# Encoder trunk on one core: in the down-projections of the gated MLP, two weight chunks of each half go through Strassen's seven block products; weights come in half-chunks, and PSUM is handed out bank by bank

## The chip, the core and the metric

The kernel runs on one core of one Trainium2 chip. The engines are TensorE (PE, matrix products), VectorE (DVE), ScalarE (ACT), GpSimd (POOL) and SyncE (SP, which here issues most of the transfers). The metric is the device time of one execution in microseconds (us); lower is better. Before the change three runs gave 2313.19, 2313.24 and 2313.95 us; the median is 2313.24.

## What is computed

A trunk of two layers on 256 tokens of width 2048. Layer 0 has grouped-query attention (mixer A), layer 1 a mixture of dilated windows (mixer B); a gated MLP of inner width 5632 follows each. All of it is float32.

```python
h = x
for i in range(DEPTH):                       # DEPTH = 2
    hn = rms_norm(h, mix_norm[i])
    h = h + (mixer_a if i % 2 == 0 else mixer_b)(hn, ...)
    h = h + conv_ffn(rms_norm(h, ffn_norm[i]), w_up[i], conv_w[i], conv_b[i], w_down[i])
return rms_norm(h, final_norm)

def conv_ffn(h, w_up, conv_w, conv_b, w_down):
    u = h @ w_up                             # 2048 -> 2 x 5632
    u = depthwise_conv_over_positions(u, conv_w, width 3) + conv_b
    gate, val = split(u)
    return (silu(gate) * val) @ w_down       # 5632 -> 2048
```

## The kernel before

**Products.** Float32 accuracy is made of three products of a rounded format: a weight tile `raw` is rounded on ACT to `wh`, DVE subtracts to get the rest `wl`, and activations are kept as a pair of tiles in the same way (`xh` and `xl`, for the MLP's inner values `ah` and `al`). Each K tile of 128 rows then takes wh by xh, wl by xh and wh by xl. The stationary operand is the activation, 128 tokens wide (token block m = 0 or 1); the moving operand is a weight row of 512 columns (n = 0 to 3 for the 2048 outputs); the sum lies in one PSUM bank of 128x512.

**Weights.** A chunk `kg` is 512 rows by 512 columns, 1 MB. `feed` (L114) loads it in one transfer on SP's queue into one of three `raw` buffers, and splits it in two half-chunks of two K tiles each. The pairs `wh`, `wl` turn in a ring of three (`NHL`). The two split instructions are placed ahead of their position in the text by `tc.high_priority(offset=AHEAD)`, 45 instructions. `feed_T` (L90) does the same for the up-projection, where the weight is the stationary operand: 16 matmuls (8 of 512 columns, 8 of 256) for each kg. Instructions of an engine run in one order, which the framework makes from the order of the text, the priorities and its own estimate of what is ready.

**The MLP** (`ffn`, L291). It runs in two halves, of six and of five groups p of 512 inner columns (`HALVES`). In each half the up-projection comes first: for each p and each hh (256 columns) the accumulators `ga` and `va`, two banks each, are fed; `up_post` (L327) takes them out of PSUM (L334 on ACT, L335 on DVE), scales, convolves, and `glu` (L353) multiplies gate by value on POOL (L354) and splits the product into `ah` and `al` (L178, L179). This side work stands in a list of generators, `pending`, of which `step()` runs one piece after each half-chunk or kg of weights. Then the half's down-projection: `project2` for n = 0 and 1 together, with the last kg of both at the end (the last product of the up-projection is still to be finished then, and `drain()` ends it before that kg), then `project` for n = 2 and n = 3. `done` adds the accumulators to the residual `h` (L273; L396 in the last half of layer 1, where the final norm follows). In a second half of layer 0 it also starts the transposes for the next layer.

**PSUM.** Eight banks: a pool of four accumulators (`accp`), taken two at a time by `new_acc`, so that a new pair takes the banks of the pair before the last; and a pool of four for everything else (`ps_tile`).

**Side inputs.** In layer 0 `bias_lines` (L664) makes bias tables beside the up-projection: small matmuls, copies to `ln` on DVE, and stores to DRAM on SP's queue (L685). In layer 1 `fin` is the final norm's gain, loaded by POOL at the start of the MLP.

## Time and profile before

| | us |
|---|---|
| median of three runs | 2313.24 |
| span of the profiled execution | 2312.0 |
| TensorE busy | 2292.1 |
| VectorE busy | 1613.9 |
| ScalarE busy | 1210.7 |
| GpSimd busy | 162.4 |
| down-projection of layer 0: first half, six chunks | from 546.6 to 677.2 |
| down-projection of layer 0: second half, five chunks | from 900.65 |
| last matmul | 2303.0 |

The profile is of one execution. A group of instructions is given by the line in the kernel, the engine, the operation and its tiles (output, arrow, inputs), with the number of instructions, their busy time, the mean duration of one in ns, and the idle time of the engine before them with what ended it. Matmuls overlap in the pipeline: the duration of one is longer than the interval at which they are issued. A row of the timeline is start, duration, engine, line, tiles, and in brackets the idle time before it and its releaser. A row of the table by stretches gives start and end, then length, and for each engine busy time and number of instructions, the granted TensorE clock, the DMA share and GB/s.

### The profile page before, as it was taken

To read this page: it belongs to the slowest core of one execution; us is meant where nothing else is said; L and a number is where in the kernel's file an instruction comes from. 1 tells how busy PE (TensorE), PEld (TensorE's weight loads), DVE (VectorE), ACT (ScalarE), POOL (GpSimd) and SP (SyncE) were. 2 spreads that over 40 slices of the span, in tenths; PEclk is the share of its full clock that TensorE was granted. 3 is DMA by queue.
4 is the path that set the end of the run, shared out by engine and by line. 5 is a ranking of instruction groups with operands and counts; after the bars stand their busy time and mean duration, and the time that the engine had idled before them with its cause. 6 is when DMAs were issued, how large, how long until landed. Compare 5 with 4: busy or idle time off the path is not lost.

```text
span 2312.0 us, 30191 instructions
## 1 busy us (share of the span) xinstructions
PE 2292.1 (99%) x11641; PEld 1946.0 (84%) x11641; DVE 1613.9 (70%) x2321; ACT 1210.7 (52%) x1746; POOL 162.4 (7%) x127
## 2 busy tenths in 40 slices
PE   9999999999999999999999999999999999999998
PEld 7788788888888888888888888878888888888886
DVE  6877877676457776778776876586777754677755
ACT  6565565554345555455454554445555543555543
POOL 2210000010000010010000000000101100001010
PEclk9999999999999999999999999999999999999999
DMA  8444565665555555565555554556555555555554
GB/s 289 156 146 148 190 201 180 229 201 194 187 195 191 191 184 189 181 222 200 195 178 174 174 198 164 172 190 212 186 191 190 191 186 198 191 191 183 193 190 146
DMA packets 229024, 437.46 MB, mean 189 GB/s; under 512 B 10400, under 2 KB 193440, under 8 KB 201104
## 3 DMA queue, kind: packets, MB, share of 16 engines
q1 hardware_dynamic: 226976, 429.82, 55.2%
q0 software_dynamic: 1472, 5.15, 0.7%
q8 instruction: 91, 1.49, 0.3%
q10 hardware_dynamic: 432, 0.56, 0.1%
q14 instruction: 53, 0.43, 0.0%
HBM read 429.20 MB, written 6.29 MB: 188 GB/s over the span
## 4 chain that ended last, share of the span: by engine, by line
PE 89%; DVE 6%; DMA 2%; issue 1%; POOL 1%; ACT 1%; SPq 1%; POOLq 0%; DVEq 0%; ACTq 0%
PE acc L107 26%; PE acc L128 15%; PE acc L129 15%; PE acc L127 15%; PE acc L110 14%; DVE wl L140 2%; DVE tT L219 2%; DMA raw<-in_w_up_dram 2%; PE ps L190 1%; PE ps L194 1%; PE ps L193 0%; PE ps L192 0%; POOL t L576 0%; SPq L685 0%; DVE h L273 0%
## 5 line engine op out<-in xcount | busy, mean ns | idle before, releaser
L140 DVE TENSOR_TENSOR wl<-raw,wh 128x1024 fp32r<-128x1024 f32 (+1 forms) x456 | 552.6, 1214 | 333.1 <-ACT wh L139 329.5
L139 ACT ACTIVATE wh<-raw 128x1024 fp32r<-128x1024 f32 (+1 forms) x456 | 475.1, 1044 | 545.6 <-PE acc L129 494.5
L107 PE MATMUL acc<-xh,wh 128*128 128x512 f32 x2816 | 707.5, 393 | 3.1 <-ACT wh L102 3.0
L107 PEld LDWEIGHTS acc<-xh,wh 128*128 128x128 f32 x2816 | 507.1, 189 | 95.7 <-ACT wh L102 4.1
L103 DVE TENSOR_TENSOR wl<-raw,wh 128x1024 fp32r<-128x1024 f32 x352 | 431.7, 1228 | 202.1 <-ACT wh L102 191.7
L102 ACT ACTIVATE wh<-raw 128x1024 fp32r<-128x1024 f32 x352 | 372.1, 1058 | 311.1 <-PE acc L107 204.4
L110 PEld LDWEIGHTS acc<-xh,wl 128*128 128x128 f32 x2816 | 384.1, 190 | 27.5
L128 PE MATMUL acc<-wl,ah 128*128 128x512 f32 x1024 | 400.1, 391 | 2.5 <-DVE wl L140 2.2
L127 PE MATMUL acc<-wh,ah 128*128 128x512 f32 x1024 | 399.2, 390 | 0.0
L129 PE MATMUL acc<-wh,al 128*128 128x512 f32 x1024 | 398.8, 389 | 0.0
L110 PE MATMUL acc<-xh,wl 128*128 128x256 f32 x2816 | 392.6, 282 | 0.0
L127 PE MATMUL acc<-wh,xh 128*128 128x512 f32 x768 | 302.3, 394 | 0.9 <-ACT wh L139 0.9
L128 PE MATMUL acc<-wl,xh 128*128 128x512 f32 x768 | 300.3, 391 | 2.2 <-DVE wl L140 2.1
L129 PE MATMUL acc<-wh,xh 128*128 128x512 f32 x768 | 299.6, 390 | 0.0
L128 PEld LDWEIGHTS acc<-wl,ah 128*128 128x128 f32 x1024 | 192.3, 188 | 46.5 <-DVE wl L140 7.6
L127 PEld LDWEIGHTS acc<-wh,ah 128*128 128x128 f32 x1024 | 192.3, 188 | 39.7
L129 PEld LDWEIGHTS acc<-wh,al 128*128 128x128 f32 x1024 | 192.3, 188 | 39.4
L354 POOL TENSOR_TENSOR cv<-cg,cv 128x512 f32<-128x512 f32 x44 | 95.5, 2170 | 1165.4 <-DVE cv L346 975.4
L128 PEld LDWEIGHTS acc<-wl,xh 128*128 128x128 f32 x768 | 144.4, 188 | 32.6 <-DVE wl L140 5.3
L129 PEld LDWEIGHTS acc<-wh,xh 128*128 128x128 f32 x768 | 144.2, 188 | 29.9
L127 PEld LDWEIGHTS acc<-wh,xh 128*128 128x128 f32 x768 | 144.4, 188 | 29.4 <-ACT wh L139 1.7
L178 ACT ACTIVATE ah<-cv 128x256 fp32r<-128x256 f32 x88 | 32.0, 411 | 105.1 <-POOL cv L354 105.1
(152 smaller groups left out, 1374.8 us busy)
## 6 DMA issues: line engine op xcount, KB each, us to landing
raw<-in_w_up_dram SPq DMA_DIRECT2D x352, 512.0 KB
raw<-in_w_down_dram SPq DMA_DIRECT2D x88, 1024.0 KB
raw<-in_w_b_dram SPq DMA_DIRECT2D x72, 1024.0 KB
raw<-in_w_bo_dram SPq DMA_DIRECT2D x24, 1024.0 KB
raw<-in_w_a_dram SPq DMA_DIRECT2D x16, 1024.0 KB
raw<-in_w_ao_dram SPq DMA_DIRECT2D x16, 1024.0 KB
raw<-in_w_a_dram SPq DMA_DIRECT2D x16, 256.0 KB
raw<-in_w_a_dram SPq DMA_DIRECT2D x8, 512.0 KB
```

The lines of the kernel that those rows point to most:

```text
L102: nc.scalar.activation(wh, rk, AF.Copy)
L103: nc.vector.tensor_tensor(wl, rk, wh.bitcast(F32), ALU.subtract)
L107: nc.tensor.matmul(acc[j], wh[:, kt, j * P:(j + 1) * P], lhs[4 * kg + kt][2], start=first and i == 0 and kt == 0, stop=False)
L110: nc.tensor.matmul(acc[j][:, :NT], wl[:, kt, j * P:(j + 1) * P], lhs[4 * kg + kt][0], start=False, stop=end and kt == 3)
L127: nc.tensor.matmul(accs[m], xh[:, c], wh[:, j, :], start=st, stop=False)
L128: nc.tensor.matmul(accs[m], xh[:, c], wl[:, j, :], start=False, stop=False)
L129: nc.tensor.matmul(accs[m], xl[:, c], wh[:, j, :], start=False, stop=sp)
L139: nc.scalar.activation(wh[:, c], r[:, c], AF.Copy)
L140: nc.vector.tensor_tensor(wl[:, c], r[:, c], wh[:, c].bitcast(F32), ALU.subtract)
L178: nc.scalar.activation(hi, src, AF.Copy)
L219: nc.vector.transpose(o[cols].rearrange("p a (m t) -> p a m t", m=2)[:, :, :, rows], s[rows].rearrange("p m (a c) -> p a m c", c=P)[:, :, ...
L354: nc.gpsimd.tensor_tensor(cv, cg, cv, ALU.mult)
```

## The change

A chunk of the inner values is a matrix of 2 token blocks by 2 K halves, and the weights of a chunk for two n are 2 K halves by 2 columns of blocks. Multiplied directly that is 8 block products, of 6 matmuls each (2 K tiles, 3 products). The changed kernel does the chunks 0 and 2 of each half (`SKG`) by a form of Strassen's scheme with 7 block products: four raw half-chunks are summed in place on DVE (`prepare`), the activations are held in seven forms, sums and differences of their blocks, each split in a pair (`glu_forms`), and the products M1, M5, M6, M7 have banks of their own beside C11, C12, C21, C22, eight in all. `combine` puts the four M into the residual. This is done for n = 0, 1 in both halves, and for n = 2, 3 in the first half only; in the second halves n = 2 and n = 3 go through `project` as before, from the forms that are the plain blocks (an eighth form is added there).

The seven P units of a Strassen chunk are mixed with the four units c of a chunk multiplied directly, in the order `MIX`; chunks that are left follow as c units: eight in a first half, four in a second. In the pair (0, 1) `drain()` stands before the last four units.

Beside that: `raw` is six half-chunks with a list of free ones, loaded by transfers of half the size, everywhere in the kernel; the `wh`, `wl` ring gets a fourth pair while a down-projection runs (tags `wh9`, `wl9`, which bias_lines uses before); banks are named, accumulators take 0 to 3 by turns of two and `ps_tile` 4 to 7; `fin` is loaded in four parts at the last down-projection, into tiles of the up-projection's input; `bias_lines` uses tiles of the MLP's pool, and one `ln` in place of two.

The diff, cut to its core:

```diff
-NRAW, NHL = 3, 3
+NRAW, NHL = 6, 3
+SKG = (0, 2)
+MIX = (("P", 1), ("c", 0), ("P", 2), ("P", 5), ("c", 1), ("P", 3), ("P", 7), ("c", 2), ("P", 6), ("P", 4), ("c", 3))
...
-    accp = ctx.enter_context(tc.tile_pool(name="accp", bufs=4, space=PS))
-    psp = ctx.enter_context(tc.tile_pool(name="psp", bufs=4, space=PS))
+    psp = ctx.enter_context(tc.tile_pool(name="psp", bufs=1, space=PS))
...
+    def bank(i, name):
+        return psp.tile([P, 512], F32, tag=f"b{i}", name=nm(name))
...
+        bank_at[1] = (bank_at[1] + 1) % 4
+        return bank(4 + bank_at[1], "ps")
...
+    def split_raw(r, release=True):
+        wh, wl = new_hl()
+        with tc.high_priority(offset=AHEAD):
+            nc.scalar.activation(wh, r, AF.Copy)
+            nc.vector.tensor_tensor(wl, r, wh.bitcast(F32), ALU.subtract)
+        if release:
+            done_raw(r)
+        return wh, wl
...
     def new_acc():
-        return [accp.tile([P, 512], F32, tag="acc", name=nm("acc")) for _ in range(2)]
+        bank_at[0] = (bank_at[0] + 2) % 4
+        return [bank(bank_at[0] + m, "acc") for m in range(2)]
...
+    def project_pair(w, n0, n1, lhs, forms, units, late, early_done, n0_done):
+        home = {1: "M1", 2: "C11", 3: "C12", 4: "C21", 5: "M5", 6: "M6", 7: "M7"}
+        place = ("M1", "M5", "M6", "M7", "C11", "C21", "C12", "C22")
+        acc = {k: bank((4, 5, 6, 7, 0, 1, 2, 3)[i], "acc") for i, k in enumerate(place)}
...
+        sums = {5: ("11", "12"), 7: ("12", "22"), 6: ("22", "11"), 4: ("21", "22")}
...
+        def prepare(u):
+            kind, kg, p = u
+            if kind == "P" and p in sums:
+                dst, src = (block(kg, b) for b in sums[p])
+                with tc.high_priority(offset=AHEAD):
+                    nc.vector.tensor_tensor(dst, dst, src, ALU.add)
+                if p == 6:
+                    done_raw(blocks.pop((kg, "11")))
+                elif p == 4:
+                    done_raw(blocks.pop((kg, "22")))
+
+        last_s = max(i for i, u in enumerate(units) if u[0] == "P")
+        for i, (kind, kg, p) in enumerate(units):
+            if i == late:
+                drain()
+            if kind == "c":
+                r = load_raw(w, (n0, n1)[p // 2], kg, p % 2)
+            else:
+                b = {1: "11", 2: "21", 3: "22", 5: "11", 7: "12", 6: "22", 4: "21"}[p]
+                r = block(kg, b)
+            if i + 1 < len(units):
+                prepare(units[i + 1])
+            wh, wl = split_raw(r, kind == "c" or p in (7, 4))
...
+            for k, xh, xl, j in todo:
+                nc.tensor.matmul(acc[k], xh, wh[:, j, :], start=k in fresh, stop=False)
+                fresh.discard(k)
+                nc.tensor.matmul(acc[k], xl, wh[:, j, :], start=False, stop=False)
+            todo.sort(key=lambda t: (t[0], t[3]))
+            for k, xh, xl, j in todo:
+                nc.tensor.matmul(acc[k], xh, wl[:, j, :], start=False, stop=last[k] == i and j == 1)
+            if i == last_s:
+                early_done(acc)
+            if i == last["C21"]:
+                n0_done(acc)
+            step()
...
+            def glu_forms(cg, cv, fm, hh):
+                nc.gpsimd.tensor_tensor(cv, cg, cv, ALU.mult)
+                yield
...
+                if hh == 0:
+                    kept[0] = cv
+                    put(1, cv[:, :, :P])
+                    if 0 in fm:
+                        put(0, cv[:, :, P:])
+                    s3 = tmp()
+                    nc.vector.tensor_tensor(s3, cv[:, :, :P], cv[:, :, P:], ALU.subtract)
+                    yield
+                    put(7, s3)
+                    return
+                c0 = kept.pop(0)
+                s1, s2, s4 = tmp(), tmp(), tmp()
+                nc.vector.tensor_tensor(s1, cv[:, :, P:], c0[:, :, P:], ALU.subtract)
+                put(2, cv[:, :, :P])
+                nc.vector.scalar_tensor_tensor(s2, s1, -1.0, c0[:, :, :P], ALU.mult, ALU.subtract)
+                yield
+                put(5, s1)
+                put(4, cv[:, :, P:])
+                nc.vector.tensor_tensor(s4, cv[:, :, :P], s2, ALU.add)
+                yield
+                put(6, s2)
+                put(3, s4)
...
-                done(project2(wd, 0, 1, slots, list(range(np_)), 1, lambda a: done(a, 0)), 1)
-                for n in (2, 3):
-                    done(project(wd, n, slots, list(range(np_)), last and hf == 1 and n == 3), n)
+                if last and hf == 1:
+                    for n in range(4):
+                        f = hpool.tile([P, 512], F32, tag=f"x{n}", name=nm("fin"))
+                        nc.gpsimd.dma_start(f, final_norm[n * 512:(n + 1) * 512].partition_broadcast(P))
+                        fin.append(f)
+                ckg = [k for k in range(np_) if k not in SKG]
+                units = []
+                for k in SKG:
+                    c = ckg.pop(0)
+                    units += [("c", c, u[1]) if u[0] == "c" else ("P", k, u[1]) for u in MIX]
+                units += [("c", c, i) for c in ckg for i in range(4)]
+                hl_ring.insert(0, (fp, 9))
...
+                def combine(acc, n0, n1):
+                    u, v = (fp.tile([P, 512], F32, tag="v", name=nm("cu"), bufs=2) for _ in range(2))
+                    nc.scalar.activation(u, acc["M1"], AF.Copy)
+                    nc.vector.tensor_tensor(hcol(0, n0), acc["M1"], hcol(0, n0), ALU.add)
+                    yield
+                    nc.vector.tensor_tensor(u, acc["M6"], u, ALU.add)
+                    nc.vector.tensor_tensor(v, acc["M5"], u, ALU.add)
+                    yield
+                    nc.vector.tensor_tensor(u, acc["M7"], u, ALU.add)
+                    nc.vector.tensor_tensor(hcol(0, n1), hcol(0, n1), v, ALU.subtract)
+                    yield
+                    nc.vector.tensor_tensor(hcol(1, n0), hcol(1, n0), u, ALU.add)
+                    yield
+                    nc.vector.tensor_tensor(u, acc["M5"], u, ALU.add)
+                    nc.vector.tensor_tensor(hcol(1, n1), hcol(1, n1), u, ALU.subtract)
+
+                def pair(n0, n1, late):
+                    acc = project_pair(wd, n0, n1, slots, forms, units, len(units) - 4 if late else None,
+                                       lambda a: start(combine(a, n0, n1)),
+                                       lambda a: done((a["C11"], a["C21"]), n0))
+                    done((acc["C12"], acc["C22"]), n1)
+
+                pair(0, 1, True)
+                if hf == 0:
+                    pair(2, 3, False)
+                else:
+                    seq = [k for k in range(np_)]
+                    for n in (2, 3):
+                        done(project(wd, n, slots, seq, last and hf == 1 and n == 3), n)
+                hl_ring.remove((fp, 9))
```

More of the change, by code (lines that the diff above doesn't have):

```diff
@@ L185, in split_scaled, with at @@
         nc.vector.scalar_tensor_tensor(lo, src, sc, hi.bitcast(F32), ALU.mult, ALU.subtract)
+    def at(e, m):
+        return e[m] if isinstance(e, list) else tuple(t[:, m * P:(m + 1) * P] for t in e[:2])
     def mm3(o, lhsT, rhs, ls, rs, start, stop):
@@ new lines, in ffn @@
+                for p in range(p0, p1):
+                    if p - p0 in SKG:
+                        fm = forms[p - p0] = {f: new_form() for f in (1, 7, 2, 5, 4, 6, 3) + (0,) * hf}
+                        if hf:
+                            for kt in range(4):
+                                slots[4 * (p - p0) + kt] = [
+                                    tuple(t[:, kt % 2 * P:(kt % 2 + 1) * P] for t in fm[f])
+                                    for f in ((1, 0), (2, 4))[kt // 2]]
+                    else:
+                        slots.update({4 * (p - p0) + j: new_form() for j in range(4)})
```

149 lines of the change are left out of this document (101 added, 48 removed).

## The prediction

> **What bounds the kernel now.** I read the page first: busy shares, the clock in the slices, the chain that ended last.
>
> ```profile
> span 2312.0 us, 30191 instructions
> PE 2292.1 (99%) x11641; PEld 1946.0 (84%) x11641; DVE 1613.9 (70%) x2321; ACT 1210.7 (52%) x1746; POOL 162.4 (7%) x127
> PEclk9999999999999999999999999999999999999999
> PE 89%; DVE 6%; DMA 2%; issue 1%; POOL 1%; ACT 1%; SPq 1%; POOLq 0%; DVEq 0%; ACTq 0%
> ```
>
> PE is busy 99% of the span at the full clock and carries 89% of the chain. So a matmul less is worth its issue interval, provided that nothing else leaves PE idle. Next I cut out the down-projection of layer 0's first half, and its groups.
>
> ```profile
> 546.60:677.20 130.60, 130.60 (x578) 108.15 (x577) 66.31 (x64) 52.39 (x54) 2.17 (x1) 1.00 0.57 193
> L127 PE MATMUL acc<-wh,ah 128*128 128x512 f32 x192 | 74.7, 389 | 0.0
> L128 PE MATMUL acc<-wl,ah 128*128 128x512 f32 x192 | 74.7, 389 | 0.0
> L129 PE MATMUL acc<-wh,al 128*128 128x512 f32 x192 | 74.7, 389 | 0.0
> L140 DVE TENSOR_TENSOR wl<-raw,wh 128x1024 fp32r<-128x1024 f32 x46 | 56.4, 1226 | 60.8 <-ACT wh L139 60.7
> L139 ACT ACTIVATE wh<-raw 128x1024 fp32r<-128x1024 f32 x46 | 48.8, 1061 | 72.7 <-PE acc L129 70.0 <-PE acc L107 1.7 <-ACT cv L339 0.7
> ```
>
> The first row gives length, then busy time of PE, PEld, DVE, ACT, POOL, then clock, DMA share, GB/s. 3x192 = 576 matmuls fill 130.6 us with PE never idle: 0.2267 us each (389 ns is the latency of one; they overlap). One half-chunk (2 K tiles, two token blocks, 3 products) is 12 matmuls, 2.72 us. ACT rounds it (1.061), DVE subtracts (1.226), and ACT then waits for PE to give a buffer back: the splits run a whole ring ahead, and DVE is used 66.31 of 130.60 us.
>
> **What it takes off PE.** A chunk with two n is 48 matmuls directly and 7 block products x 6 = 42 by Strassen's scheme. Two chunks in each pair of n; pairs (0,1) and (2,3) in a first half, only (0,1) in a second: 3 pairs x 2 chunks x 2 layers = 12 times 6 = 72 matmuls, 72 x 0.2267 = **16.3 us**. The six matmuls of a product go to one bank in a row; three in a row do now at that same interval, so I keep it (no run of six is in the trace; in the up-projection the banks alternate, and four 512-wide matmuls there, in a row below, take 1.07 us, 0.39 for one and (1.07-0.39)/3 = 0.227 for each more, so either order costs the same).
>
> **What it adds to the splits.** Eleven units (7 P, 4 c) are 42 + 48 = 90 matmuls, 20.4 us. DVE gets 11 subtractions and 4 sums of raw blocks. A sum in place of that size is in the trace, in mixer A:
>
> ```profile
> L578 DVE TENSOR_TENSOR ro<-ro,t 128x1024 f32<-128x1024 f32 x5 | 6.1, 1217 | 0.8 <-POOL t L576 0.8
> ```
>
> 11x1.226 + 4x1.217 = 18.4 us on DVE against 20.4 us on PE, 90%. ACT has 11x1.061 = 11.7. On average DVE keeps pace, with 2.0 us to spare per stretch (pitch below: more). In detail: a P unit gives PE 1.36 us, a P with a sum asks DVE for 2.44. But the order never has more than two P together, and with the fourth hl pair a split may run three units ahead; the three units ahead of any unit hold at least one c, so at least 1.36+1.36+2.72 = 5.4 us. The chain of one unit is sum, rounding, subtraction: 1.217+1.061+1.226 = 3.5 us. I take **0** here. Its bounds are 0 and, if nothing ran ahead, the slower rival's price below. The c units behind both stretches (8 or 4) need DVE 1.23 of 2.72 us and rebuild the lead.
>
> The first pair meets the last gated product's work too. Rows of DVE, ACT and PE at the start of that stage:
>
> ```profile
> 546.62 0.40 PE L127 MATMUL acc<-wh,ah 128*128 128x512 f32 x1
> 545.91 1.06 ACT L139 ACTIVATE wh<-raw 128x1024 fp32r<-128x1024 f32 x1 [1.72 <-PE acc L107]
> 546.88 0.64 ACT L334 ACTIVATE v<-acc 128x256 f32<-128x256 f32 x2
> 547.01 1.23 DVE L140 TENSOR_TENSOR wl<-raw,wh 128x1024 fp32r<-128x1024 f32 x1 [1.56 <-ACT wh L139]
> 548.15 0.75 DVE L335 TENSOR_TENSOR v<-acc,v 128x256 f32<-128x256 f32 x2
> 548.93 0.69 DVE L337 TENSOR_TENSOR u<-v,rbc 128x512 f32<-128x512 f32 x1
> 551.80 0.88 DVE L344 SCALAR_TENSOR_TENSOR cv<-u,cw,cv 128x256 f32<-128x256 f32 x2
> 552.59 0.87 DVE L346 SCALAR_TENSOR_TENSOR cv<-u,cw,cv 128x256 f32<-128x256 f32 x2
> 553.43 1.23 DVE L140 TENSOR_TENSOR wl<-raw,wh 128x1024 fp32r<-128x1024 f32 x1
> 553.64 2.17 POOL L354 TENSOR_TENSOR cv<-cg,cv 128x512 f32<-128x512 f32 x1 [21.01 <-DVE cv L346]
> 556.29 0.76 DVE L179 TENSOR_TENSOR al<-cv,ah 128x256 fp32r<-128x256 f32 x2 [1.63 <-ACT ah L178]
> ```
>
> A subtraction holds DVE 547.01 to 548.15 = 1.14 us when the next follows at once, so fifteen take 17.1 us and leave 3.3. The extra work is 0.75+0.69+0.88+0.87+0.76 = 4.0 us, over two stretches with 6.6 us free. Covered. The product is wanted only by the last four units, 2 x 20.4 us later.
>
> **New wait one: the start of a pair.** Before, four accumulators rotated. Now C11 lies in bank 0, where va was, and unit c0 comes second. P1 ends at 546.62 + 1.36 = 547.98. Bank 0 is free when the first L335 is done, 548.15 + 0.38 = 548.53, and with 0.07 us for the signal (an estimate: from ACT's end, 545.91 + 1.06, to DVE's start at 547.01 it is 0.04) c0 starts at 548.60: 0.62 us late. Bank 1 is free at 548.15 + 0.75 + 0.07 = 548.97, and C11's first two matmuls have issued by 549.05: no more. Four starts: **2.5 us**. Bounds: 0, if DVE takes L335 ahead of the subtraction; (0.62+1.14) x 4 = 7.0, if a second subtraction or sum stands ahead. I take the order that the trace has. Late next is nothing: all later units shift with it, and the splits gain lead.
>
> **New wait two: the end of a pair.** C12 and C22 lie in banks 2 and 3, and the next accumulator (ga of the second half, or the acc of n = 2) takes just these. Today's end of that stage:
>
> ```profile
> 676.92 1.28 DVE L273 TENSOR_TENSOR h<-acc,h 128x512 f32<-128x512 f32 x2
> 677.21 1.07 PE L107 MATMUL acc<-xh,wh 128*128 128x512 f32 x4
> ```
>
> The residual adds take DVE from 676.92 to 678.20, 0.64 each, and PE went on at 677.21 into other banks. Now the first matmul waits for 677.56+0.07, 0.42 late. In feed_T the second writes bank 3, free at 678.27 instead of wanted at 677.86: 0.41 more. Two such ends: 1.7 us. With n = 2, three matmuls (0.68) go to bank 2 first, so 0.42; but there DVE has the combine (8 more operations like L273, 8x0.64 = 5.1 us), the C11 adds and, in layer 0, transposes, all within c3 and four c units, 13.6 us, that need 5 x 1.14 of DVE besides. That is tight, so I take 0.8 each, 1.6. Sum **3.3 us**; bounds 0 and 3.3 + 4x1.14 = 7.9 (a subtraction ahead each time). In first halves eight c units, 21.8 us, hide the combine.
>
> **What is hidden, and by what.** *Forms.* Seven or eight splits in place of four, and four sums or differences, per Strassen chunk, in the up-projection:
>
> ```profile
> 677.20:901.00 223.80, 223.80 (x1283) 196.97 (x1282) 161.55 (x233) 127.80 (x186) 20.14 (x9) 1.00 0.58 189
> ```
>
> At 0.38 us for a 256-wide DVE operation (half of L179's pair) the most is 2x(4+4)x0.38 = 6.1 us per half, in 62 us of idle DVE; without that cover, 4 x 6.1 = 24 us. *Loads.* Twice as many of half the size on SP; volume and order stay, the stage moves 193 GB/s at a DMA share of 0.57, and eight half-chunks per 20.4 us instead of 21.8 ask 7% more: 0.61. Slots: in a stretch four raws are held by blocks, and walking through the list of free ones, each load's slot was given back by a split five or more units earlier, at least 3x1.36 + 2x2.72 = 9.5 us. *fin.* Four POOL issues ahead of the last product, 4 x 0.75 = 3.0 us, hidden by the 40 us above:
>
> ```profile
> L711 POOL DMA_DIRECT2D btg<-scr x4 | 3.0, 747 | 86.8 <-DVE lg L745 86.8
> oh<-in_onehot_dram POOLq DMA_DIRECT2D x1, 512.0 KB, 3.9
> ```
>
> *bias_lines.* Its stores share SP with the weights and hold them up today:
>
> ```profile
> PE acc L107 <- ACT wh L102: 3.0, 2, 2.0
> 388.59 7.53 SPq L685 DMA_DIRECT2D scr<-ln  x4
> 396.23 9.20 SPq L95 DMA_DIRECT2D raw<-in_w_up_dram  x4
> 405.52 6.09 SPq L685 DMA_DIRECT2D scr<-ln  x4
> ```
>
> Finer raw slots could give those 3.0 us back. One ln in place of two makes DVE's next copy wait for four stores: issued 388.59 to 396.12, landed 3.9 us on (the half-megabyte row above) is 400.0, and the next stores stand at 405.5. I take 0, bounds -3 to +3.
>
> *A rule against it.* POOL's multiply by fin slows DVE subtractions from 1.23 to 2.36 us:
>
> ```profile
> 2250.92 3.23 POOL L399 TENSOR_TENSOR h<-h,fin 128x512 f32<-128x512 f32 x2 [2.58 <-ACT junk L398]
> 2252.88 2.36 DVE L140 TENSOR_TENSOR wl<-raw,wh 128x1024 fp32r<-128x1024 f32 x1 [1.12 <-ACT wh L139]
> ```
>
> At 1.13 us for the one product beside each pair's start, that fits into 3.3 us. The Trainium skill, "SBUF — State Buffer", section "Who interferes with whom", says that a DVE instruction with two SBUF inputs and a GpSimd one that reads SBUF exclude each other through a shared read port. By that rule all sums and subtractions are exposed; the trace agrees in the row above, though at 553.43 a subtraction took 1.23 beside L354 and POOL was the slow one (2.17). By the rule the sum would lose at most 4 x 2.17 us of DVE time, and by the rows it stays hidden.
>
> **Sum.** 2312.0 - 16.3 + 2.5 + 3.3 = 2301.5 us of span. The median, 2313.24, stands 1.24 above the span; added unchanged: **2302.7 us**, 0.46% faster.
>
> **Rivals.**
> *DVE holds the stretches, partly.* Fifteen operations at 1.23 plus the 4.0 and POOL's 1.13 come to 21 us in a pair's first stretch, 20.4 on PE; if the queue's order wastes another 0.5 us in each of 12, 6 us go: 2308.7, and up to 2313. For it: 84 to 90% with an engine that works in order. Against: the ring's lead, the c units.
> *The lead is lost: slower.* If sum and split of a unit start only as the unit ahead runs, PE waits 3.5 us less that unit's time: behind P2, P3 and P6 2.14 each, behind c2 0.8, 7.2 a stretch, 12 x 7.2 = 86 us: about 2389. It decides from 10.5/12 = 0.9 us a stretch on. A raw slot that comes a load late (3.9 us) once a stretch does likewise, 47 - 10.5 = 36 us slower. For it: a sum waits for two loads and stands on DVE ahead of its neighbour's subtraction. Against: ACT waiting for PE in the rows above, and the slot walk.
> *No new wait.* If the schedule frees the banks in time and the 3 us at the stores come back: 2313.24 - 16.3 - 3 = 2294, at least below 2297.
> *It does not do what it says.* Fewer chunks taken than I count is excluded by the text of the loops; 72 is a count.
>
> **How the numbers follow.** Forecast (2297 to 2308.6) 0.68; DVE partly bound 0.12, about all of it within 0.2%, 4.6 us, which is what a measurement tells from no change; lead lost 0.15; no new wait 0.05. Faster 0.73, same 0.12, slower 0.15. The range runs from 2296.9 (all 16.3, no wait) to 2311.0, far into the second case; outside remain the slow case and most of the last.
>
> **What would show it.** 11569 PE instructions. In a stretch P and c units at 1.36 and 2.72 us with PE never idle; DVE near 85%; ACT's waits still on PE. At each pair's start PE waits some 0.6 us on L335's line, at each end 0.4 to 0.8 us on a residual add. Wrong would be: PE waiting on a sum or a subtraction within a stretch, ACT waiting on DMA there, an issue interval above 0.2267, or more than 1 us lost at a pair's ends.

## The result, and the profile after

The changed kernel takes **2325.99 us** (median of four runs, 2324.59 to 2327.89); the kernel before, run beside it, 2313.3. The ratio is 1.0055, with a 95% interval of 1.0041 to 1.0069: 12.7 us slower, where 10.5 us less were forecast. The profiled execution took 2326.31 us.

The head of the page of the changed kernel: span, busy time by engine, and the granted clock by slices.

```profile
span 2324.5 us, 31224 instructions
PE 2290.6 (99%) x11569; PEld 1935.9 (83%) x11569; DVE 1751.6 (75%) x2513; ACT 1256.6 (54%) x1816; POOL 168.8 (7%) x130
PEclk9999999999999999999999999999999999999999
```

The 72 matmuls are gone (11641 - 11569), but PE's busy time fell by 1.5 us, not 16.3, and the span grew by 12.5. So matmuls became slower on average, and PE stands idle more. The page does not say where: 40 slices of 58 us hide a stall of 4. The stages do. First the table by stretches of the kernel before, for two stages that the prediction did not show, then that of the changed kernel: layer 0's first up-projection, first down-projection and second up-projection, and the last down-projection of layer 1. Columns as in the prediction.

```profile
269.35:546.62 277.27, 274.21 (x1563) 239.94 (x1561) 200.33 (x299) 155.33 (x232) 25.41 (x21) 1.00 0.62 203
...
2194.44:2303.04 108.60, 108.60 (x482) 89.95 (x480) 59.02 (x59) 46.17 (x56) 11.88 (x8) 1.00 0.48 164
```

```profile
269.94:554.97 285.03, 277.43 (x1563) 242.65 (x1561) 207.02 (x316) 159.01 (x239) 27.14 (x21) 0.98 0.63 197
554.97:684.28 129.31, 128.08 (x554) 103.22 (x553) 104.51 (x107) 65.21 (x68) 3.24 (x1) 1.00 0.62 197
684.28:907.82 223.54, 223.54 (x1281) 196.73 (x1282) 168.90 (x251) 129.74 (x193) 20.14 (x9) 1.00 0.61 188
2203.57:2315.57 112.00, 108.38 (x470) 87.36 (x468) 75.42 (x80) 50.67 (x62) 13.80 (x8) 1.00 0.48 157
```

The first down-projection has 24 matmuls less, 5.4 us, and became 1.3 us shorter; the last has 12 less and became 3.4 us longer; and the worst place is an up-projection in which no block product runs, 7.8 us longer and at a mean clock of 0.98. The second up-projection, where most forms are made, kept its length (223.44 to 223.54).

For each stage I took the starts of successive matmuls, subtracted 0.2267 us from each distance and sorted what is left by place. That gives the sum of the prediction again, measured:

| term, us | forecast | in the trace after |
|---|---|---|
| 72 matmuls less | -16.3 | -16.3 |
| one `ln` (first up-projection) | 0 (-3 to +3) | +7.8 |
| issue interval in the down-projections | 0 | +6.6 |
| start of a pair, four | +2.5 | 0.50 + 0.62 + 0.76 + 2.87 = +4.8 |
| end of a pair, four | +3.3 | 0.58 + 2.19 + 0.58 + 0.58, and 1.6 at half clock = +5.5 |
| the last product of each half, four | 0 | 4 x 1.22 = +4.9 |
| waits that the kernel before had in layer 0's second half | not counted | -1.4 |
| the rest | 0 | +0.6 |
| sum | -10.5 | +12.5 |

**One `ln`.** Rows of the changed kernel around the first stores of bias lines: DVE, then SP's queue, then PE.

```profile
395.73 0.69 DVE L888 COPY ln<-ps 128x512 f32<-128x512 f32 x1 [9.63 <-DMA scr<-ln]
...
397.39 1.22 DVE L120 TENSOR_TENSOR wl<-raw,wh 128x1024 fp32r<-128x1024 f32 x1
```

```profile
379.99 3.06 SPq L891 DMA_DIRECT2D scr<-ln  x4
383.16 6.62 SPq L134 DMA_DIRECT2D raw<-in_w_up_dram  x2
```

```profile
393.39 2.00 PE L143 MATMUL acc<-xh,wh 128*128 128x512 f32 x8
398.66 1.65 PE L146 MATMUL acc<-xh,wl 128*128 128x256 f32 x6 [3.27 <-DVE wl L120]
```

The four stores were issued by 383.05, and the copy into the same `ln` started at 395.73: 12.7 us. Until then DVE, which works in order, does nothing for 9.63 us; the subtractions behind the copy are late, and PE runs dry. It happens again at 423. The DMA view of the changed kernel for 376 to 396 us, in slices of 0.5 us (busy tenths of the 16 engines, GB/s), with the loads' median time to landing in that window:

```profile
DMA  7974789403799333222322239994258993222222
GB/s 207 340 254 131 213 285 360 143 23 123 213 307 318 115 68 78 70 70 90 86 53 78 78 102 268 360 381 162 102 170 285 360 363 125 102 92 98 96 98 96
raw<-in_w_up_dram SPq DMA_DIRECT2D x4, 512.0 KB, 11.1
```

From 382.5 us on there are stretches with two to three tenths of the engines busy and 53 to 125 GB/s, against 197 in the stage as a whole. Four stores of 256 KB are 1.05 MB, 8 us and more at such a rate (an estimate), and the loads beside them took 11.1 us to land too.

The trace also holds when the parts of each transfer were complete (no view prints this; it is worked out from the trace's semaphore records). The last parts of the four stores were complete at 387.6, 390.3, 392.9 and 395.4 us: the stores went one after the other, 2.6 us each. A load behind them, issued at 383.16, had twelve of its sixteen parts by 390.1 and the last four only at 395.7 to 396.8. The kernel before has the same: its first four stores, issued by 383.1, were complete at 386.2, 389.0, 391.6 and 394.2. So the change did not slow the stores; it made DVE stand behind them. The copies of the kernel before, into its other `ln`:

```profile
385.10 0.69 DVE L682 COPY ln<-ps 128x512 f32<-128x512 f32 x1
397.93 0.42 DVE L682 COPY ln<-ps 128x256 f32<-128x256 f32 x1
```

With one `ln` the first of them would have had to wait 9.1 us, from 385.10 to 394.2, and the second as long, for a group of stores that was complete at 407.1.

**The idle time can also cost clock.** The table by stretches of the changed kernel:

```profile
390.00:400.00 10.00, 6.73 (x37) 5.71 (x36) 4.24 (x8) 2.04 (x3) 0.00 (x0) 0.92 0.37 120
400.00:410.00 10.00, 10.00 (x54) 8.69 (x54) 8.15 (x14) 6.08 (x10) 2.11 (x1) 0.91 0.66 216
...
420.00:430.00 10.00, 5.67 (x29) 4.83 (x29) 4.96 (x10) 2.05 (x3) 0.29 (x1) 0.79 0.58 173
430.00:440.00 10.00, 10.00 (x52) 8.59 (x51) 8.77 (x17) 6.75 (x13) 1.82 (x1) 0.87 0.68 212
```

0.08 + 0.09 of 10 us lost is 3.4 us at half clock at the first gap, 0.21 + 0.13 is 6.8 us at the second. Both stretches begin before PE starts again: at 398.40 for a start at 398.66, and at 425.71 for a start at 428.01. So PE worked 3.2 and 4.5 us at half clock and lost 1.6 and 2.3 us of work; with 7.6 us idle that is 11.5 us.

**The last product of a half.** Rows of POOL, ACT and PE in the first pair:

```profile
564.85 3.24 POOL L465 TENSOR_TENSOR cv<-cg,cv 128x512 f32<-128x512 f32 x1 [23.88 <-DVE cv L457]
568.13 0.73 ACT L288 ACTIVATE ah<-cv 128x256 fp32r<-128x256 f32 x2 [4.54 <-POOL cv L465]
568.76 4.83 ACT L119 ACTIVATE wh<-raw 128x1024 fp32r<-128x1024 f32 x5
572.93 0.40 PE L273 MATMUL acc<-wh,al 128*128 128x512 f32 x1
573.94 0.51 PE L276 MATMUL acc<-wl,ah 128*128 128x512 f32 x1 [0.61 <-DVE wl L120]
```

ACT's rounding of the product stands in its queue ahead of the weights' and waits 4.54 us for POOL; then five roundings of weights follow in one go: ACT is caught up, but the lead of the splits is gone. Units P6 and P4 lose 0.30 and 0.92 us, alike to 0.1 us in all four first pairs. POOL took 3.24 us here and 2.17 before. In the kernel before the same product takes 1.28 us where no DVE operation with two SBUF inputs runs beside it (at 418.25), and 2.16 to 2.24 in most places, where a subtraction lies beside it for 1.0 to 1.1 us; here a subtraction and a sum do for 2.2 us. So it is longer by about the time that such operations of DVE run beside it.

**Start and end of a pair.** The two worst places. Layer 1's last half, DVE, then PE:

```profile
2204.52 1.22 DVE L240 TENSOR_TENSOR raw<-raw,raw 128x1024 f32<-128x1024 f32 x1 [2.49 <-DMA raw<-in_w_down_dram]
2205.66 2.35 DVE L120 TENSOR_TENSOR wl<-raw,wh 128x1024 fp32r<-128x1024 f32 x2
2207.94 0.41 DVE L446 TENSOR_TENSOR v<-acc,v 128x256 f32<-128x256 f32 x1
```

```profile
2205.42 0.39 PE L271 MATMUL acc<-wh,ah 128*128 128x512 f32 x1
2208.41 0.50 PE L271 MATMUL acc<-wh,ah 128*128 128x512 f32 x1 [2.60 <-DVE v L446]
```

A sum waits for its load, two subtractions follow, and only then DVE empties the bank that C11 needs. At the end of layer 0's pair, DVE, then PE:

```profile
961.57 1.78 DVE L332 STREAM_TRANSPOSE tT<-h 32x256 f32<-32x256 f32 x4
963.38 1.29 DVE L386 TENSOR_TENSOR h<-acc,h 128x512 f32<-128x512 f32 x2
```

```profile
964.22 0.48 PE L164 MATMUL acc<-wh,ah 128*128 128x512 f32 x1 [2.02 <-DVE h L386]
...
965.40 0.63 PE L165 MATMUL acc<-wl,ah 128*128 128x512 f32 x1
965.82 0.63 PE L166 MATMUL acc<-wh,al 128*128 128x512 f32 x1
```

Four transposes stand ahead of the residual adds that free banks 2 and 3; from 965.00 on, matmuls start 0.427 us apart, at half clock, for 3.4 us.

**The issue interval.** In some places where PE waits for nothing, matmuls start 0.233 us apart and not 0.2267. The prediction had named such an interval as a sign against it. Which operands it goes with is the subject of four experiments.

### The profile page after: what moved, and what is told of

It reads as the page before. It is cut to its first block, busy times and chain, and to the rows that moved or that the text cites. A ratio compares the mean times of both kernels' runs of the same rounds, so it can differ in the third digit from the quotient of the medians.

```text
span 2324.5 us, 31224 instructions
## 1 busy us (share of the span) xinstructions
PE 2290.6 (99%) x11569; PEld 1935.9 (83%) x11569; DVE 1751.6 (75%) x2513; ACT 1256.6 (54%) x1816; POOL 168.8 (7%) x130
## 4 chain that ended last, share of the span: by engine, by line
PE 89%; DVE 5%; DMA 1%; issue 1%; ACT 1%; POOL 1%; SPq 0%; POOLq 0%; DVEq 0%; ACTq 0%
PE acc L143 27%; PE acc L146 14%; PE acc L165 11%; PE acc L166 11%; PE acc L164 11%; PE acc L271 4%; PE acc L273 4%; PE acc L276 4%; DVE wl L120 2%; DVE tT L332 1%; ACT wh L119 1%; DMA scr<-ln 1%; PE ps L303 1%; POOL cv L465 1%; PE ps L307 1%
## 5 line engine op out<-in xcount | busy, mean ns | idle before, releaser
L119 ACT ACTIVATE wh<-raw 128x1024 fp32r<-128x1024 f32 x828 | 872.7, 1058 | 779.3 <-PE acc L166 284.3
L120 DVE TENSOR_TENSOR wl<-raw,wh 128x1024 fp32r<-128x1024 f32 x828 | 1014.1, 1230 | 363.5 <-ACT wh L119 349.9
L271 PE MATMUL acc<-wh,ah 128*128 128x512 f32 x520 | 204.7, 394 | 3.6 <-DVE v L446 3.6
L273 PE MATMUL acc<-wh,al 128*128 128x512 f32 x520 | 204.3, 393 | 0.0
L164 PE MATMUL acc<-wh,ah 128*128 128x512 f32 x480 | 188.8, 393 | 2.4 <-DVE h L386 2.0
L165 PE MATMUL acc<-wl,ah 128*128 128x512 f32 x480 | 189.2, 394 | 2.0 <-DVE wl L120 1.8
L166 PE MATMUL acc<-wh,al 128*128 128x512 f32 x480 | 187.8, 392 | 0.0
L276 PE MATMUL acc<-wl,ah 128*128 128x512 f32 x520 | 148.0, 393 | 2.5 <-DVE wl L120 2.5
L271 PEld LDWEIGHTS acc<-wh,ah 128*128 128x128 f32 x520 | 97.6, 188 | 27.2 <-DVE v L446 5.4
L276 PEld LDWEIGHTS acc<-wl,ah 128*128 128x128 f32 x520 | 97.0, 188 | 27.1 <-DVE wl L120 5.9
L273 PEld LDWEIGHTS acc<-wh,al 128*128 128x128 f32 x520 | 97.6, 188 | 21.8
L165 PEld LDWEIGHTS acc<-wl,ah 128*128 128x128 f32 x480 | 90.6, 189 | 24.2 <-DVE wl L120 5.8
```

Source lines behind the costliest of these rows:

```text
L119: nc.scalar.activation(wh, r, AF.Copy)
L120: nc.vector.tensor_tensor(wl, r, wh.bitcast(F32), ALU.subtract)
L164: nc.tensor.matmul(accs[m], xh, wh[:, j, :], start=st, stop=False)
L165: nc.tensor.matmul(accs[m], xh, wl[:, j, :], start=False, stop=False)
L166: nc.tensor.matmul(accs[m], xl, wh[:, j, :], start=False, stop=sp)
L271: nc.tensor.matmul(acc[k], xh, wh[:, j, :], start=k in fresh, stop=False)
```

## The experiments

The theory after this reading: five separate losses, none of them in the block products' arithmetic. The rivals: the losses hang together (repair one, and DVE or ACT takes it back elsewhere), and the long interval belongs to the block products themselves or to DVE's load beside them.

### Two `ln` tiles in the changed kernel

```diff
-                ln = lp.tile([P, 512], F32, tag="junk", name=nm("ln"))
+                ln = lp.tile([P, 512], F32, tag="ln", name=nm("ln"), bufs=2)
```

> The changed kernel with two ln buffers in bias_lines again, nothing else. Theory (DVE's copy into the one ln waits for the four stores of the copy before, 18.7 us in three waits, and holds up the weight splits queued behind it on DVE): the first up-projection of layer 0, 285.0 us now and 277.3 before the change, comes back to 277 to 278, and the whole goes from 2326.0 to about 2318.3. Rival (the half-chunk slots and half-size loads on SP beside the stores are what starves the splits there): that stage stays above 283, the whole above 2324.

Measured: 2316.52 us, ratio to before 1.0015 (1.0005 to 1.0024): 9.5 us less than with one. The stage, in the table by stretches of this kernel:

```profile
269.00:542.30 273.30, 273.30 (x1563) 239.74 (x1562) 208.13 (x316) 158.88 (x239) 26.32 (x21) 1.00 0.65 205
```

PE has no idle time left, the clock is whole, and the stage is 11.7 us shorter than with one `ln` and 4 us shorter than in the kernel before. The wait on the stores was the cause, and the single `ln` also hid a gain. Not all of the 11.7 us came through: in this profile the last down-projection took 114.55 us in place of 112.00, with a longer wait at the start of its pair and 3.4 us at half clock behind it. The rival of this run was weak in one point: the up-projections' loads have 512 KB in both kernels (352 of them), so it is the slots that became finer there, not the transfers.

### One `ln` tile in the kernel before

```diff
-                ln = lp.tile([P, 512], F32, tag="ln", name=nm("ln"), bufs=2)
+                ln = lp.tile([P, 512], F32, tag="ln", name=nm("ln"), bufs=1)
```

> The kernel before with one ln buffer in place of two, nothing else. Theory of the single ln: the first up-projection of layer 0 goes from 277.3 to 283 or more, the whole from 2313.3 to 2319 to 2322. Rival (half-chunk loads are at fault): within 1 us of 2313.3.

Measured: 2317.31 us, ratio 1.0019 (1.0010 to 1.0029), 4.3 us slower; the stage grew from 277.3 to 281.3 us, and DVE waited 16.1 us on the stores, three times. So such a loss needs nothing else of the change. Its size does: 4.0 us of the stage here, 11.7 in the changed kernel, and the 283 us or more that the theory expected did not come. Two parts of the difference are on record: the kernel before already lost some 3 us at the same stores (the row with ACT in the prediction), and here the gaps, up to 2.83 us between matmul starts, cost no clock, where the changed kernel lost 3.9 us of work.

### C11 and C21 in the banks that come free first

```diff
-        acc = {k: bank((4, 5, 6, 7, 0, 1, 2, 3)[i], "acc") for i, k in enumerate(place)}
+        acc = {k: bank((4, 5, 6, 7, 2, 3, 0, 1)[i], "acc") for i, k in enumerate(place)}
```

Now C12 and C22, which begin later and end last, use the banks that va has just left, and the accumulator that follows finds the banks of C11 and C21, long since added.

> The changed kernel with C11, C21 in banks 2, 3 and C12, C22 in banks 0, 1, nothing else. Theory (PE loses 4.7 us at the four starts of a pair (0,1), waiting for va to be taken out of banks 0 and 1, and about 5.7 us at the four ends, waiting for the residual adds out of banks 2 and 3, half-clock time after the longest wait included): all of these gaps go, the whole falls by 9 to 10.5, to about 2316. Rival (DVE is behind in these places anyway, with 16 sums per pair, and PE would wait for splits in place of banks): waits of PE on wl or wh appear in their place and the gain is under 4 us.

Measured: 2316.25 us, ratio 1.0014 (1.0004 to 1.0023): 9.7 us less than the changed kernel. In the waits of PE no bank is named any more, at the start or at the end. What is left in the first down-projection:

```profile
PE acc L276 <- DVE wl L120: 0.2, 1, 0.2
```

Waits and half clock by my sorting had come to 4.8 + 5.5 = 10.3 us at starts and ends; 9.7 came back. Some of that is the lead that the splits keep: the gap at P6 and P4 shrank too (0.5 us in that stage in place of 1.2). So the two terms aren't cleanly separate. The median hides a spread: the ten runs lie between 2313.66 us, at a mean granted clock of 0.998, and 2318.24 us at 0.996.

### The last product of each half on DVE

```diff
-            def glu(cg, cv, slots, k0):
-                nc.gpsimd.tensor_tensor(cv, cg, cv, ALU.mult)
+            def glu(cg, cv, slots, k0, eng=None):
+                (eng or nc.gpsimd).tensor_tensor(cv, cg, cv, ALU.mult)
...
-                            return glu(cg, cv, slots, 4 * kg + 2 * hh)
+                            return glu(cg, cv, slots, 4 * kg + 2 * hh, nc.vector if final and hh else None)
```

> The changed kernel with the last gate-by-value product of each half on DVE in place of POOL, nothing else. Theory (POOL's multiply takes 3.24 us beside the sums and subtractions, ACT stands behind it with the roundings of five later units in its queue, and units P6 and P4 of the first stretch start 1.2 us late, four times): both gaps of 0.3 and 0.9 us at units 8 and 9 go in all four halves, the whole falls by 4 to 5, to about 2321.3. Rival (these two units are late since DVE itself has no room for sum and subtraction there): 0.7 us more on DVE keeps or widens the gaps, the whole stays within 1 us of 2326.0 or rises.

Measured: 2322.70 us, ratio 1.0038 (1.0024 to 1.0052), 3.3 us less, where 4 to 5 were expected. In its profile the four down-projections are 4.3 us shorter together, and the first up-projection, which the edit does not touch, took 286.2 us in place of 285.0. The product, on DVE:

```profile
566.98 0.68 DVE L465 TENSOR_TENSOR cv<-cg,cv 128x512 f32<-128x512 f32 x1
```

0.68 us in place of 3.24, in a queue that was held to be the tight one; the gaps at P6 and P4 are gone. DVE had room for it, and PE's loss had come through ACT's wait for POOL. Whether that was due to POOL's 3.24 us in place of 2.17, or to ACT's order alone, this run does not separate.

### The three together

> The three repairs together: two ln tiles, banks of the first correction sums moved to those that come free early, last product of each half on DVE. Theory (three separate losses): the gains add, 9.5 + 9.7 + 3.3 us off 2326.0, 2303.5 us, between 2302 and 2305, ratio to before 0.9955 to 0.9965; the first up-projection stage 273.2 us, the down-projection of layer 0's first half 126.7 or less, and units 8 and 9 without gaps. Rival (the losses overlap: what one repair frees, DVE or ACT takes back at the next place, above all in the last half, where DVE's sum waits for its load): 2307 us or more, with waits of 1 us and more left in the last half.

Measured: 2301.97 us (2300.39 to 2302.83), ratio **0.9951** (0.9939 to 0.9964): faster than before. The single gains sum to 9.5 + 9.7 + 3.3 = 22.5 and the kernel gained 24.0: they add, within the runs' spread. The rival falls, though something of it shows: in the last half waits of 2.7 us are left. In the other three down-projections of the MLP PE waits for nothing at all, yet the first takes 127.1 us for 552 matmuls, where 552 x 0.2267 is 125.1. That is the interval.

### Which matmuls are slow: the tiles in the MLP's pool handed out first

Of 30 form pairs 24 lie in the pool that lives through the kernel (hpool) and six in the MLP's own (fp), as does the fourth pair of split tiles. The units 22 to 25 of the changed kernel's first pair, c units all, by the row with which each starts, and the start of unit 26:

```profile
597.88 0.39 PE L271 MATMUL acc<-wh,ah 128*128 128x512 f32 x1
600.60 0.40 PE L271 MATMUL acc<-wh,ah 128*128 128x512 f32 x1
603.39 0.40 PE L271 MATMUL acc<-wh,ah 128*128 128x512 f32 x1
606.18 0.39 PE L271 MATMUL acc<-wh,ah 128*128 128x512 f32 x1
608.98 0.39 PE L271 MATMUL acc<-wh,ah 128*128 128x512 f32 x1
```

Unit 22 lasts 2.72 us (12 x 0.2267), the others 2.79 or 2.80 (12 x 0.233): 23 and 25 read their slots in fp, 24 has the fourth weight pair.

```diff
-                tags = iter([(hpool, k) for k in range(24)] + [(fp, k) for k in range(24, 30)])
+                tags = iter([(fp, k) for k in range(24, 30)] + [(hpool, k) for k in range(24)])
```

> As the three repairs, but the six form pairs that lie in the MLP pool are handed out first instead of last, so that six products of the first stretch read them, and the last chunk's slots lie in the other pool. Theory A (the matmul's interval depends on where its operand lies): the 233 ns move with the tiles: units 26 to 29 of the first half go back to 227 ns wherever their weights do not lie in the MLP pool, and the products P1, P2, P5, P7, P6 and P4 of the first stretch go to 233; 72 slow form matmuls of a pair become 36, some 0.2 us less in a pair, below what the time can tell. Theory B (the interval belongs to the place in the sequence, the last units, where the next stage's loads and the combination run): units 26 to 29 stay at 233 and the first stretch at 227.

Measured: 2301.25 us, ratio 0.9947 (0.9933 to 0.9961). The same units:

```profile
585.47 0.39 PE L271 MATMUL acc<-wh,ah 128*128 128x512 f32 x1
588.19 0.39 PE L271 MATMUL acc<-wh,ah 128*128 128x512 f32 x1
590.91 0.40 PE L271 MATMUL acc<-wh,ah 128*128 128x512 f32 x1
593.70 0.39 PE L271 MATMUL acc<-wh,ah 128*128 128x512 f32 x1
596.43 0.39 PE L271 MATMUL acc<-wh,ah 128*128 128x512 f32 x1
```

Only unit 24 is slow now, with the fourth weight pair; 23 and 25 take 2.72 and 2.73. In the same way units 27 and 29 went from 233 to 227 and 228 ns a matmul, and the products P2, P5 and P7 of the first stretch, at 227, 226 and 227 with the three repairs alone, came to 233, 232 and 233. The slow interval moved with the tiles, though not cleanly: many units that read nothing there but stand behind one that does took 228 to 232 ns, here and with the three repairs alone. The time, as expected, can't tell the two kernels apart.

### Three pairs of split tiles

```diff
-                hl_ring.insert(0, (fp, 9))
...
-                hl_ring.remove((fp, 9))
```

> As the three repairs, but without the fourth pair of split tiles in the MLP pool, so that three pairs serve the down-projections. Theory A (every fourth unit is slow because its weights lie in the MLP pool): those units go to 227 ns, about 100 matmuls of each of the four pairs by 6 ns, 2.5 us off, about 2301 us, if three pairs are enough. Rival (the fourth pair is the cover of the split): the intervals are 227 all the same, but PE waits for the splits inside the stretches, 1.36 us of matmuls in a product unit against a split of 0.7 + 1.2 us and more, and the time is 2305 us or more.

Measured: 2300.62 us, ratio 0.9947 (0.9934 to 0.9961). Units are no longer slow by fours; those with slots in fp stay at 233 ns, and the others that wait for nothing are at 227, but for a few at 228 to 232. The excess over 0.2267 in the four down-projections fell from 6.8 to 3.6 us, and waits for the splits rose from 2.7 to 4.0, so both theories have a part. The time gained, 1.4 us, is less than the two kernels' runs scatter.

### Finer slots without block products, and with the fourth pair

Half-chunk slots, halved loads, named banks, two `ln` and three pairs of split tiles, while the down-projections are multiplied directly:

```diff
-SKG = (0, 2)
+SKG = ()
...
-                pair(0, 1, True)
-                if hf == 0:
-                    pair(2, 3, False)
...
+                done(project2(wd, 0, 1, slots, list(range(np_)), 1, lambda a: done(a, 0)), 1)
+                for n in (2, 3):
+                    done(project(wd, n, slots, list(range(np_)), last and hf == 1 and n == 3), n)
```

> The changed kernel's half-chunk slots, halved loads and named banks, with two ln tiles and without block products: the down-projections are multiplied directly, six matmuls a block, with three pairs of split tiles. Theory (the finer slots take away the stalls behind the bias stores, and the block products have no part in that): the first up-projection stage is 273 to 274 us against 277.3, the down-projections 130.6 and 108.6 as before, in all 3.5 to 4 us off 2313.1, about 2309.4. Rival (that gain comes with the forms, whose side work shifts the order around the stores, or the halved loads cost elsewhere what they give here): the stage stays at 277 us, or the time at 2313 or above.

Measured: 2312.02 us, ratio 0.9996 (0.9987 to 1.0005). The two stages:

```profile
268.93:544.31 275.38, 274.02 (x1563) 239.91 (x1561) 199.21 (x299) 155.38 (x232) 26.31 (x21) 1.00 0.64 204
544.31:674.89 130.58, 130.58 (x578) 108.15 (x577) 66.30 (x64) 52.37 (x54) 2.17 (x1) 1.00 0.62 192
```

The down-projection is as before to 0.01 us, so halved loads cost nothing. The up-projection lost 1.9 of the 4.0 us: the finer slots do about half of it, and the other half comes only with the forms; that their side work gives a better order is likely, but not shown. The expectation of 273 to 274 us missed.

The same with the fourth split pair in fp (the two `hl_ring` lines kept):

> As the slots alone, with a fourth pair of split tiles in the MLP pool while a down-projection runs. The pair is not needed here, since three pairs already keep the splits ahead. Theory A (a matmul's interval is longer when its operand lies in the MLP pool): every fourth half-chunk of a down-projection runs at 232 or 233 ns a matmul, 576 / 4 = 144 matmuls by 6 ns, 0.8 to 0.9 us more on the 130.6 us of the first half, though no block product is left in it. Theory B (the longer interval belongs to the block products, their order of banks or DVE's load beside them): 227 ns throughout, 130.6 us.

One run, 2315.71 us, too few to compare times. Starts of four half-chunks in a row:

```profile
554.37 0.39 PE L164 MATMUL acc<-wh,ah 128*128 128x512 f32 x1
...
557.09 0.40 PE L164 MATMUL acc<-wh,ah 128*128 128x512 f32 x1
...
559.88 0.39 PE L164 MATMUL acc<-wh,ah 128*128 128x512 f32 x1
...
562.60 0.39 PE L164 MATMUL acc<-wh,ah 128*128 128x512 f32 x1
```

2.72, 2.79, 2.72, then two more of 2.72: each fourth is slow through all 48, and the stage takes 131.45 us in place of 130.59, the 0.86 expected. No block product, no sum and no crowded DVE is left in this kernel. Theory B falls. In layer 1 theory A is not exact either: each fourth half-chunk takes 234 ns a matmul there, and the one behind it 229 with neither operand in fp.

### The tiles in the MLP's pool read least

Three repairs, three split pairs, tiles in fp handed out first (the edits of the sections above together).

> The three repairs, three pairs of split tiles, and the form pairs in the MLP pool handed out first, so that the tiles there are read by six matmuls of a pair of n each, and not by twelve. Theory (the rate of the operand's pool is all that is left inside the pairs): 36 slow matmuls in a pair in place of 48 to 72, and none by the fourth weight pair; the excess over 227 ns in the four down-projections falls from 3.6 us (ring of three) to some 2.3, and the time to 2299.5, between 2298.5 and 2300.5. Rival (three pairs are too few once the first products are slower): waits for the splits of more than 2 us in all, 2301 us or more.

Measured: **2299.58 us** (2298.31 to 2301.75), ratio **0.9941** (0.9928 to 0.9953): 13.4 us faster than the kernel before, the best of all. The excess over 0.2267 is 2.4 us in the four down-projections; 3.8 us of waits remain in the two second halves, more than the rival's 2 us, but the time is the theory's. Mean distance of the matmul starts in units of the first pair, in ns, worked out from the trace, beside the kernel with three split pairs and the tiles in fp handed out last:

```
unit        P2   P5   P7   P6   P4    c26  c27  c29
tiles last  227  227  227  227  227   233  233  233
tiles first 233  232  233  233  232   227  227  227
```

The first and the last down-projection in the table by stretches:

```profile
542.70:668.44 125.74, 125.74 (x554) 103.58 (x553) 104.67 (x108) 66.48 (x69) 0.00 (x0) 1.00 0.63 205
2179.20:2287.52 108.32, 107.06 (x470) 87.39 (x468) 77.36 (x82) 52.02 (x63) 9.41 (x7) 1.00 0.51 165
```

The first down-projection is 4.9 us shorter than before (24 matmuls make 5.4), with DVE busy 104.67 of 125.74 us.

## Why the prediction was wrong

**The largest miss was `bias_lines`**, held at 0 with bounds of 3 us: "issued 388.59 to 396.12, landed 3.9 us on (the half-megabyte row above) is 400.0, and the next stores stand at 405.5". Three things failed in it. The 3.9 us were those of one load on POOL's queue, used for four stores among weight loads; these stores were complete 11 us after their last issue, in the kernel before too (407.1, not 400.0). The step asked when the next stores come, 405.5, where the next copy into the tile stood at 397.93. And it did not ask who stands behind the waiting copy: DVE's subtractions, and PE behind them. 7.8 us against the kernel before, 9.5 us back when undone. The bound should have been what DVE waits, 9 us twice. No term alone turned the sign: with this one undone the kernel still took 2316.52 us, 3.5 more than before; the three repairs together bring it below.

**"The product is wanted only by the last four units"** was true for PE and false for ACT, where its rounding stands in order among the weights' roundings. 4.9 us by the trace after, 3.3 us back in the time.

**"three in a row do now at that same interval, so I keep it"** looked at the order of banks, which made no difference: products of six in one bank do run at 0.227 us with operands outside fp. (The trace before had longer runs, against the prediction's word: the last 24 matmuls of layer 1 go to one bank twelve at a time, 0.2267 us apart.) What the change altered was where operands lie: forms and a split pair in the MLP's pool. 6.6 us, where the prediction had 0 and no bound.

**The waits for banks were seen, and under-sized**: 5.8 us forecast (bounds 0 and 14.9), 10.3 by the trace, 9.7 back with the banks swapped. Their mechanism, va's evacuation at the start and the residual adds at the end, was right. A sum that stands on DVE for its load (2.87 us in one start) was named in a rival only; the transposes ahead of the residual adds were named and priced at 0.4 us more, where the end took 2.19; the half clock behind a gap was missing. The stated range was too narrow for its own bounds as well: 14.9 us of waits and 3 at the stores put its top at 2314.8, not 2311.0.

**Right**: 72 matmuls and 11569 PE instructions; the forms (0.1 us in the second up-projection); the halved loads; the slot walk; 15 sums and subtractions a stretch beside PE. With three repairs PE waits for nothing in three of the four down-projections. *DVE holds the stretches* and *The lead is lost* both fell as causes there: DVE's own work did not hold these three, though the lead was lost for the length of two units each time that ACT stood behind POOL. In the fourth, 2.7 us of waits for the splits are left. *No new wait* fell at once.

The rule from the Trainium skill that the prediction weighed, "SBUF — State Buffer", section "Who interferes with whom", did hold: POOL's product of two SBUF inputs went from 2.17 to 3.24 us beside DVE's sums. I had priced it as DVE time (4 x 2.17 us, hidden); it was paid through POOL's delay, by ACT and PE.

That the three repairs together came to 2301.97 us, beside the 2302.7 forecast, does not save the sum: it holds 6.8 us of long intervals and 2.7 of waits that the forecast did not have, and 3.6 us won in the first up-projection that it had put at 0.

## What to carry to other kernels

When a buffer is taken away, price the wait by the engine that will stand in it: what is queued behind the waiting instruction, and for how long, from the row of just that transfer or with a wide bound. A result that is "needed late" still blocks the queue in which its next step stands, so look at its consumer's neighbours too. And when accumulators trade places, give the banks that come free first to the sums that begin first.

## What the runs showed of the hardware

*The pool of an operand goes with the matmul's interval.* In the down-projections 128x512 matmuls of this format start 0.2267 us apart with both operands in the kernel-long pools, and mostly 0.232 to 0.234 us apart when either the moving operand (a split pair) or the stationary one (a form) lies in the MLP's pool; with both there it is 0.229 to 0.233. It follows the tiles when they are handed out in another order, and shows with no block product around. It is not the whole rule. Many units behind such a one take 0.228 to 0.232 with nothing there, and in the up-projections of the kernel before, with both operands in kernel-long pools, the first five of eight 512-wide matmuls in a row start 0.228 to 0.238 us apart on average, and only the last three 0.227. Whether it is the address, a neighbour or something else is not tried.

*POOL and DVE hold each other up.* POOL's product of two SBUF inputs took 1.28 us alone, 2.24 with a DVE subtraction beside it for 1.1 us, and 3.24 with a subtraction and a sum beside it for 2.2 us. Once, at 321.75 in the kernel before, it kept its 1.29 us, and the subtraction that began 0.17 us behind it took 2.2 in place of 1.23.

*Stores went one after the other.* Four stores of 256 KB on SP's queue were complete 2.6 us apart, the last 11 to 12 us after its issue, in both kernels.

*Short gaps can cost clock.* With a gap of 2.4 us between matmul starts the clock was halved for 3.4 us, with one of 4.7 us for 6.8. Not each gap does it: 2.99 us in the same trace (from 2205.42, in the rows above) cost no clock, nor did 2.42 us in the run with the last product on DVE, at the very place that cost 3.4 us in the changed kernel; there 2.97 us at the start of the last pair did. The Trainium skill, "TensorE: Matmul & The Clock Gate", part 1, has the clock halved after an idle window of about 3.4 us and restored after a busy one of the same length. The lengths at half clock agree with that window; the gap that set it off was shorter than one here, so a stall of 2 us can cost 1.6 us more than itself.
